# A chunk-streaming layer on one core: a new hand-written order for the mixed stages, with a re-fitted planner

## The chip, the cores and the metric

The kernel runs on one core of a Trainium2 chip. The metric is the device time of one execution in microseconds (us). The engines are TensorE (PE, with its weight loads shown apart as PEld), VectorE (DVE), ScalarE (ACT), GpSimd (POOL) and SyncE (SP), which here issues nearly all DMAs.

## The reference, cut to what matters

One layer of an encoder is computed for 512 prompt tokens and 32 sample tokens together (544 columns), in float32, with weights split in two rounded parts (high and low) so that each product takes three matmuls.

```python
xn = rms_norm(x, norm1)
q, k, v, iq, ik, iw, u, g_a, g_b = split(xn @ w_in)
# sparse attention: index scores, top-k keys per query, softmax over those keys
score = einsum(relu(iq . ik), iw);  top_k(score, n_sel);  o_a = softmax(q . k_sel) @ v_sel
# RWKV-7 time mixing: token shift, decay, a delta-rule state carried over chunks of tokens
y_b, shift_new, wkv_new = rwkv_time_mix(u, ...)
h = x + (sigmoid(g_a) * (o_a @ w_oa) + sigmoid(g_b) * (y_b @ w_ob)) @ w_out
h = h + (silu(rms_norm(h) @ w_gate) * (rms_norm(h) @ w_up)) @ w_down
y = rms_norm(h, norm_f)
```

Prompt queries choose 128 of up to 512 keys; sample queries choose 256 of 1056. The 16 index heads have 64 channels each; attention has 8 heads; the RWKV part has 8 heads, worked in four pairs.

## The kernel before, in words

Two kinds of work follow one another. In the *mixed stages* the input projection is done in 128-wide blocks, and between its matmuls lie all the small steps of attention and of RWKV. In the *late* part (merge, output projection, feed-forward) there are only large matmuls and their evictions.

**A weight block.** `wblock` (lines 246 to 265) loads 128 output columns of a weight matrix into one of two `raw` buffers (L255, a DMA on SP), copies the rounded high part with ACT (L256) and takes the low part with DVE (L260). Three `hi`/`lo` buffers go round. `gemm` multiplies a block with the 544 columns in two halves of 272, each 24 matmuls into one PSUM bank (L279), then evicts.

**The steps of the mixed stages.** `build` walks through the string `ORDER` (L67 to L70), whose words are steps, and emits each step's instructions:

- `U0` to `U3`: three projection blocks each for one RWKV pair (`u_pair`, `u_tile`, evictions L761 and L762, a shift on DVE at L767), stored to DRAM (L795). `L` is the first projection, of the LoRA inputs. From the word `U1` on, the projections use only PSUM banks 0 and 1.
- `P0` to `P3`: the preparation of one pair (`rwkv_prep`, L804 on), many small steps on every engine. `C0` to `C3`: the chain over nine chunks of tokens (`chain_step`, L1058 to L1071) and what follows it (`rwkv_post`, L1104 to L1143).
- `KV`, `IQ`, `Q`, `G0,16`: the projections of keys and values, index queries (eight blocks, stored to `iq_dram` at L467), queries (four blocks, stored to `q_dram` at L475) and gates (sixteen blocks, stored to `gate_dram` at L1150).
- `CI2`, `CI0,1`: cached keys of the sample stream brought in.
- `SI`: the sample index (`sample_index`, L477). After the scores it finds 256 keys per query by a bisection of 34 rounds (`topk_sample`); each round is a count on DVE (L529) and a small matmul over partitions (L530), and each waits for the one before.
- `X1` to `X3`: the selection for the second, third and fourth block of 128 prompt queries (`prompt_index`, L591): four query loads (L450, in `queries`), scores (L458, L459), relu on ACT (L604), a weighted sum over 16 heads on DVE (L611), then 16 rounds of a maximum of eight (L615) and a replacement (L616). The first block needs no selection. `FI` frees their buffers.
- `A0` to `A3`, `AS`: attention of the four prompt blocks and of the sample (`attend_prompt`, L629; scores with a maximum on DVE at L645; exponentials at L649; the output stored to `o_dram` at L680 except for the last). `UO`, `M`, `MA0`, `MA1`: the state output, the move to the merge, and the attention side of the merge for each half of the tokens.

**What shared buffers make of the order.** `queries` takes the next of two buffers (`qraw`, `qhs`) for its loads, and the scores take the next of two PSUM banks (`ab`). `SI`, `X`, `A`, `AS` and `CI` share them, in the order in which they are emitted. So the query loads of a step wait until the step emitted two loads earlier has used its own. `X1` to `X3` share one accumulator (`acc`), so each waits for the selection before it. `SI`, `A` and `AS` share the buffers `p_r` and `pT_r`, which `X` does not use.

**The planner.** The program is built twice. After the first build `plan` and `schedule` (L1602 on) run a list scheduling on the host: each instruction has a priority from the place where it was emitted plus a number of its group from the table `SHIFT` (lower goes first; a `w` before a name means that step's weight blocks), and costs, hand-over times between engines (`HOP`) and DMA times are constants in the file. The second build fixes the order that came out on each engine. `hold` and `keep` are added when PE would leave the full or a smaller tile shape; `turn` is added when an engine would change its starting partition, and where it is not in the table it is zero. Dependencies come from the emitted order, and the planner cannot go past them.

Of the kernel before, what the change touches and what calls it, by code (L numbers as in the profile page):

```python
# [35 lines left out]
def _consts():  # L36
# [28 lines left out]
B_COLS = 7432  # L65
ACT_COLS = 22 * 2 * T
ORDER = (  # L67
    "L U0 KV P0 IQ IA CI2 SI U1 P1 C0 X1 U2 P2 C1 Q A0 X2 U3 P3 C2 A1 CI0,1 AS X3 FI "
    "A2 G0,16 UO M MA0 C3 A3 MA1 "
)  # L70
SHIFT = {
# [7 lines left out]
    17100, "wstart": -230000,  # L79
}  # L80
BUSY = 1 << 40
AGE = 24
# [1385 lines left out]
def unlayout(r):  # L1468
# [6 lines left out]


HOP = {("PE", "Activation"): 200, ("PE", "DVE"): 200, ("PE", "Pool"): 225, ("DVE", "PE"): 149, ("Activation", "PE"): 160, ("Pool", "PE"): 174,
       ("Activation", "DVE"): 142, ("DVE", "Activation"): 128, ("DVE", "Pool"): 155, ("Activation", "Pool"): 210, ("Pool", "Activation"): 250,
       ("Pool", "DVE"): 70, ("DVE", "DVE"): 127, ("Pool", "Pool"): 104, ("Activation", "Activation"): 60, ("PE", "PE"): 0}
SECOND = {"PE": 54, "Activation": 70, "DVE": 70, "Pool": 48, "SP": 0}  # L1480
TURN = {"Activation": 128, "DVE": 110, "Pool": 112}
ENGINES = ("PE", "Activation", "DVE", "Pool", "SP")
WINDOW = 4096 / 1.2
ROUNDED, WHOLE, TURNED = 0, 1, 2
# [45 lines left out]
def side(i):  # L1530

    a = next((x for x in i.outs if hasattr(x, "ap")), None)
    step = list(a.ap)[0][0] if a is not None else 0
    return a.offset // step if step else 0


def port(i):
# [64 lines left out]
def plan(K, instructions):  # L1602

    at, group, g = {}, [], iter(K.groups + [(len(instructions), None)])
    block = [False] * len(instructions)
    for a, b in K.blocks:
        block[a:b] = [True] * (b - a)
    nxt, cur = next(g), "start"
    L, prio = [], []
    for n, i in enumerate(instructions):  # L1610
        while nxt and nxt[0] <= n:
            cur, nxt = nxt[1], next(g, None)
        if not i.opcode.startswith("Tile") and i.opcode != "Ldweights":
            at[i.name] = len(L)
            L.append(i)
            group.append(("w" if block[n] else "") + cur)
            prio.append(i.bass_priority + SHIFT.get(group[-1], 0))
    succ, need, reach = [[] for _ in L], [0] * len(L), []
    for k, i in enumerate(L):
        seen = 0  # L1620
        for p in sorted({at[x] for d in re.findall(r"deps=\[([^\]]*)\]", i.concise(deps=True)) for x in d.split(",") if x in at}, reverse=True):
            if p < k and not seen >> p & 1:
                succ[p].append(k)
                need[k] += 1
                seen |= reach[p] | 1 << p
        reach.append(seen)
    engine, dma, work = [str(i.engine)[11:] for i in L], [i.opcode == "DMACopy" for i in L], [cost(i) for i in L]
    sides = [0 if x or e in ("PE", "SP") else side(i) for x, e, i in zip(dma, engine, L)]
    return L, group, prio, succ, need, engine, dma, work, bundles(succ, group, engine, work, reach), sides


# [22 lines left out]
def schedule(L, group, prio, succ, need, engine, dma, work, runs, sides):  # L1654
    need, shared = list(need), [port(i) for i in L]
    missing, late, members = {}, {}, {}
# [4 lines left out]
    hold, keep, turn = SHIFT.get("hold", 0), SHIFT.get("keep", 0), SHIFT.get("turn", 0)  # L1661
    names = [e for e in ENGINES if e in engine]
    free, order, here = dict.fromkeys(names, 0.0), {e: [] for e in names}, {e: {} for e in names}
# [6 lines left out]
    array, queue, bus, left, at = Array(), 0.0, 0.0, len(L), dict.fromkeys(names, 0)  # L1670
# [22 lines left out]
    while left:  # L1693
# [3 lines left out]
        while coming and coming[0][0] <= t + 1e-6:  # L1697
            k = heapq.heappop(coming)[1]
# [4 lines left out]
        for e in names:  # L1703
            while free[e] <= t + 1e-6:
                if e == "PE":
# [4 lines left out]
                    k = heapq.heappop(tiles[best[1]])[1]  # L1710
                else:
# [3 lines left out]
                    k = heapq.heappop(here[e][best[1]])[1]  # L1715
# [8 lines left out]
                for p in before[k]:  # L1724
                    x, v = mark[p]
# [3 lines left out]
                t0 = max(t, ready[k] + SECOND[e]) if len(waits) > 1 else t  # L1729
                began = t0  # L1730
                if dma[k]:
                    queue = max(t0 + 67, queue + 25) + 450
                    bus = max(queue + 650, bus) + work[k]
                    end, free[e] = bus, t0 + 60
                elif isinstance(work[k], tuple):
                    began, end = array.run(t0, *work[k])
                    free[e] = max(began + 1, t0 + 1)
# [56 lines left out]
```

## Time and profile before

| what | value |
|---|---|
| median of 3 runs | 1007.6 us (1006.28 to 1008.33) |
| profiled execution, device time | 1007.89 us |
| its span, first to last instruction | 1006.1 us |
| mean granted TensorE clock | 0.985 |
| PE busy | 964.9 us, 96% of the span |
| DVE busy | 628.1 us, 62% |
| ACT busy | 460.0 us, 46% |
| POOL busy | 190.4 us, 19% |
| HBM traffic | 110 GB/s over the span |

The profiled execution lies 0.3 us above the median of the runs. Its device time holds 1.8 us outside the span. A share of busy time over the whole span mixes two parts: up to about 515 us the mixed stages run, after it the late part.

### The profile page before, as it was taken

What the parts mean: (1) busy time and instruction counts of PE and PEld (TensorE: products, weight loads), DVE (VectorE), ACT (ScalarE), POOL (GpSimd) and SP (SyncE); (2) the same over time, 40 slices, a digit from 0 to 9 for tenths busy, and PEclk for the clock granted to TensorE, in tenths of its full rate; (3) what the DMA queues carried; (4) which work ended last, traced back from release to release, by engine and by line L of the source; (5) the groups of instructions that cost most, each with busy time, mean ns of one, the idle gap of its engine ahead of it and who ended that gap; (6) DMA issues with size and microseconds to landing.
All of it is one profiled execution on the core that took longest, in us unless ns stands there. A gap on an engine that the chain in (4) does not pass through costs nothing.

```text
span 1006.1 us, 20829 instructions
## 1 busy us (share of the span) xinstructions
PE 964.9 (96%) x8268; PEld 923.4 (92%) x8268; DVE 628.1 (62%) x1452; ACT 460.0 (46%) x965; POOL 190.4 (19%) x307
## 2 busy tenths in 40 slices
PE   6989999999989999999999999999999999999996
PEld 5979997898879887899899999999999999999995
DVE  5947635999999898799677654444444444313132
ACT  6644555465546876565734452222323222223231
POOL 2212213322423421220000231111111111011112
PEclk9999999899999998999999999999999999999998
DMA  6246332432343455343555322232222233223222
GB/s 229 84 119 193 113 101 64 126 115 88 122 133 106 144 172 142 120 129 94 153 154 188 122 84 85 87 99 89 84 85 84 85 89 95 72 87 96 79 74 89
DMA packets 63282, 112.58 MB, mean 112 GB/s; under 512 B 13616, under 2 KB 33872, under 8 KB 63056
## 3 DMA queue, kind: packets, MB, share of 16 engines
q1 hardware_dynamic: 62144, 110.72, 35.7%
q8 instruction: 65, 1.06, 0.5%
q10 hardware_dynamic: 1040, 0.52, 0.2%
q14 instruction: 33, 0.27, 0.1%
HBM read 93.67 MB, written 17.14 MB: 110 GB/s over the span
## 4 chain that ended last, share of the span: by engine, by line
PE 72%; DVE 14%; DMA 6%; ACT 4%; issue 2%; SPq 1%; POOL 0%; DVEq 0%; ACTq 0%; POOLq 0%
PE bank L279 49%; PE bank L1330 13%; PE bank L458 1%; DVE w L260 1%; DVE f L616 1%; PE bank L459 1%; DMA iq_dram<-f 1%; DMA raw<-in_w_x_dram 1%; DVE f L611 1%; DVE f L615 1%; PE bank L901 1%; DVE f L529 1%; ACT w L256 1%; PE bank L1058 1%; DVE f L928 1%
## 5 line engine op out<-in xcount | busy, mean ns | idle before, releaser
L279 PE MATMUL bank<-r,w 128*128 128x272 f32 x4752 | 658.3, 293 | 3.2 <-ACT f L762 2.8
L279 PEld LDWEIGHTS bank<-r,w 128*128 128x128 f32 x4752 | 617.3, 189 | 10.0 <-ACT f L762 3.5
L256 ACT ACTIVATE w<-raw 128x1024 fp32r<-128x1024 f32 (+1 forms) x135 | 137.8, 1021 | 223.6 <-PE bank L279 172.7
L260 DVE TENSOR_TENSOR w<-raw,w 128x1024 fp32r<-128x1024 f32 (+1 forms) x135 | 176.5, 1308 | 97.8 <-ACT w L256 97.6
L1330 PE MATMUL bank<-r,w 128*128 128x272 f32 x1056 | 133.0, 288 | 0.0
L1330 PEld LDWEIGHTS bank<-r,w 128*128 128x128 f32 x1056 | 132.4, 188 | 0.0
L1308 POOL TENSOR_TENSOR f<-f 128x544 f32<-128x544 f32 x22 | 30.4, 1382 | 234.0 <-DVE f L1305 224.9
L1305 DVE TENSOR_TENSOR f<-bank,f 128x272 f32<-128x272 f32 x44 | 19.4, 442 | 74.8 <-PE bank L279 74.8
L1298 DVE TENSOR_TENSOR f<-bank,f 128x272 f32<-128x272 f32 x44 | 19.1, 435 | 45.1 <-PE bank L279 45.1
L453 POOL TENSOR_TENSOR k<-f,k 64x512 fp32r<-64x512 f32 (+1 forms) x22 | 30.1, 1372 | 49.0 <-ACT k L452 43.4
L458 PE MATMUL bank<-k 128*128 128x512 f32 (+5 forms) x102 | 35.8, 359 | 3.1 <-DVE f L645 1.3
L1332 DVE TENSOR_TENSOR f<-bank,f 128x272 f32<-128x272 f32 x16 | 7.1, 442 | 47.7 <-PE bank L1330 47.7
L1336 POOL TENSOR_TENSOR f<-f 128x272 f32<-128x272 f32 x13 | 12.4, 955 | 110.8 <-ACT f L1334 110.8
L459 PE MATMUL bank<-k 128*128 128x512 f32 (+5 forms) x102 | 33.0, 333 | 0.0
L1334 ACT ACTIVATE f<-f 128x272 f32<-128x272 f32 x16 | 6.8, 423 | 57.1 <-DVE f L1332 57.1
L1299 ACT ACTIVATE f<-f 128x272 f32<-128x272 f32 x44 | 18.7, 424 | 29.8 <-DVE f L1298 29.8
L611 DVE SCALAR_TENSOR_TENSOR f<-f,f 128x256 f32<-128x256 f32 (+2 forms) x45 | 31.7, 705 | 0.9 <-ACT f L604 0.3
L279 PE MATMUL bank<-k,w 128*128 128x272 f32 x144 | 22.8, 322 | 9.8 <-ACT k L300 9.8
L279 PEld LDWEIGHTS bank<-k,w 128*128 128x128 f32 x144 | 21.6, 219 | 10.1 <-ACT k L300 9.7
L458 PEld LDWEIGHTS bank<-k 128*128 128x128 f32 x102 | 19.1, 188 | 10.7 <-issue 5.1
L1074 POOL COPY f<-f 64x64 f32<-64x64 f32 x56 | 16.3, 292 | 65.3 <-DVE f L1071 63.9
L1250 POOL TENSOR_TENSOR f<-f 128x272 f32<-128x272 f32 x14 | 12.5, 896 | 75.3 <-DMA raw<-in_w_out_dram 51.7
(352 smaller groups left out, 1239.0 us busy)
## 6 DMA issues: line engine op xcount, KB each, us to landing
raw<-in_w_x_dram SPq DMA_DIRECT2D x41, 512.0 KB, 3.7
raw<-in_w_gate_dram SPq DMA_DIRECT2D x22, 512.0 KB, 3.6
raw<-in_w_up_dram SPq DMA_DIRECT2D x22, 512.0 KB, 3.6
raw<-in_w_down_dram SPq DMA_DIRECT2D x16, 512.0 KB, 3.6
gate_dram<-f SPq DMA_DIRECT2D x16, 272.0 KB, 2.4
raw<-in_w_oa_dram SPq DMA_DIRECT2D x8, 512.0 KB, 3.8
raw<-in_w_out_dram SPq DMA_DIRECT2D x8, 512.0 KB, 3.7
f<-iq_dram SPq DMA_DIRECT2D x26, 128.0 KB, 2.8
```

Of the source, the lines that this page charges most:

```text
L256: nc.scalar.activation(hi[:, a], raw[:, a], AF.Copy)
L260: self.lo_eng.tensor_tensor(lo[:, b], raw[:, b], hif[:, b], op=OP.subtract)
L279: nc.tensor.matmul(o, a[:, k], c[k][:, s], start=n == 0, stop=n == 3 * nk - 1)
L453: nc.gpsimd.tensor_tensor(ql[0:64], raw[0:64], qh_r.v(512)[0:64, :n], op=OP.subtract)
L458: nc.tensor.matmul(out, q[0][:, i:i + m], self.KS[:, j, keys], start=True, stop=False)
L459: nc.tensor.matmul(out, q[1][:, i:i + m], self.KS[:, j, keys], start=False, stop=stop)
L611: nc.vector.scalar_tensor_tensor(acc, r[:, i * S:(i + 1) * S], w, acc, op0=OP.mult, op1=OP.add)
L1298: nc.vector.tensor_tensor(t1[:, s], o, self.rs[:, s], op=OP.mult)
L1299: nc.scalar.activation(t1[:, s], t1[:, s], AF.Silu)
L1305: nc.vector.tensor_tensor(t2[:, s], o, self.rs[:, s], op=OP.mult)
L1308: nc.gpsimd.tensor_tensor(t1, t1, t2, op=OP.mult)
L1330: nc.tensor.matmul(o, a[:, k], c[k0 + k][:, s], start=m == 0, stop=m == 65)
```

## The change: what it does

In `ORDER` the second pair's projection `U1` stands ahead of the sample index `SI`; `X2` stands right behind `X1`, where it stood behind `A0`; `X3` and `FI` stand ahead of `U3`, `P3`, `C2`, `A1`, `CI0,1` and `AS`, where they stood behind `AS`. No step is added or taken away, and no instruction's shape changes.

All numbers of `SHIFT` are replaced, and `turn` is added. In the planner's model two hand-over times of GpSimd and one cost of a partition change are changed, and SP is taken as occupied for 330 ns by each DMA that it issues, 585 ns where one side of the copy has fewer than 128 partitions (60 ns before). Ready DMAs of the two kinds are queued apart.

```diff
 ORDER = (
-    "L U0 KV P0 IQ IA CI2 SI U1 P1 C0 X1 U2 P2 C1 Q A0 X2 U3 P3 C2 A1 CI0,1 AS X3 FI "
+    "L U0 KV P0 IQ IA CI2 U1 SI P1 C0 X1 X2 U2 P2 C1 Q A0 X3 FI U3 P3 C2 A1 CI0,1 AS "
     "A2 G0,16 UO M MA0 C3 A3 MA1 "
 )
 SHIFT = {
-    "A0": 230600, "A1": -4400, "A2": -703900, "A3": -225600, "AS": -582700, "C0": 247900, "C1": -1362900, "C2": -248200,
-    "C3": 114200, "CI0,1": 41500, "CI2": -198600, "G0,16": 2588600, "IA": 213400, "IQ": 1151100, "KV": -9600, "L": 65100,
-    "M": -200900, "MA0": 308900, "MA1": 123300, "P0": 259300, "P1": -250900, "P2": -372500, "P3": -86600, "Q": 3546000,
-    "R0": 299400, "R1": -1861400, "R2": -142400, "R3": 126400, "S": -59800, "SI": 126900, "U0": -21700, "U1": 1680300, "U2":
-    227900, "U3": 188000, "UO": -131400, "X1": 2420500, "X2": 24200, "X3": -241300, "hold": -55800, "keep": 2547100, "late":
+    "A0": 189800, "A1": -337800, "A2": 674100, "A3": -448400, "AS": -316200, "C0": 469200, "C1": -2295400, "C2": -279600,
+    "C3": -159300, "CI0,1": 8600, "CI2": -32700, "G0,16": 701400, "IA": 114200, "IQ": 1093000, "KV": -26200, "L": 224200,
+    "M": -330800, "MA0": 140200, "MA1": 187900, "P0": 1046500, "P1": -43900, "P2": -330500, "P3": -125000, "Q": 2748500,
+    "R0": 1376800, "R1": -861800, "R2": 525400, "R3": 38100, "S": -30900, "SI": 300400, "U0": 6700, "U1": 1510600, "U2":
+    802000, "U3": 296000, "UO": -13700, "X1": 2558100, "X2": -70800, "X3": -64500, "hold": -118500, "keep": 2716000, "late":
...
+    255500, "start": 407400, "turn": 87400, "wG0,16": 1072700, "wIQ": 155500, "wMA0": 1299200, "wMA1": -69900, "wP0": 18100,
...
-       ("Activation", "DVE"): 142, ("DVE", "Activation"): 128, ("DVE", "Pool"): 155, ("Activation", "Pool"): 210, ("Pool", "Activation"): 250,
-       ("Pool", "DVE"): 70, ("DVE", "DVE"): 127, ...
+       ("Activation", "DVE"): 142, ("DVE", "Activation"): 128, ("DVE", "Pool"): 155, ("Activation", "Pool"): 210, ("Pool", "Activation"): 112,
+       ("Pool", "DVE"): 110, ("DVE", "DVE"): 127, ...
-TURN = {"Activation": 128, "DVE": 110, "Pool": 112}
+TURN = {"Activation": 132, "DVE": 110, "Pool": 112}
...
+def narrow(i):
+    return any(list(x.ap)[0][1] < 128 for x in list(i.outs) + list(i.ins) if hasattr(x, "ap"))
...
-    sides = [0 if x or e in ("PE", "SP") else side(i) for x, e, i in zip(dma, engine, L)]
+    sides = [32 * narrow(i) if x else 0 if e == "PE" else side(i) for x, e, i in zip(dma, engine, L)]
...
-                    queue = max(t0 + 67, queue + 25) + 450
+                    issue = 585 if sides[k] else 330
+                    queue = max(t0 + 67, queue) + issue + 120
                     bus = max(queue + 650, bus) + work[k]
-                    end, free[e] = bus, t0 + 60
+                    end, free[e] = bus, t0 + (issue if e == "SP" else 60)
```

## Rows read from the trace of the kernel before

**Rows 1.** The page: busy time of the engines over the span, share, instructions

```profile
PE 964.9 (96%) x8268; PEld 923.4 (92%) x8268; DVE 628.1 (62%) x1452; ACT 460.0 (46%) x965; POOL 190.4 (19%) x307
```

**Rows 2.** Busy time by stretch: window, its length, then the columns named first

```profile
core 0: us, PE busy (x) PEld busy (x) DVE busy (x) ACT busy (x) POOL busy (x), PEclk, DMA share, GB/s
...
60.00:160.00 100.00, 95.19 (x903) 88.48 (x901) 52.93 (x139) 50.88 (x122) 20.46 (x38) 0.98 0.41 123
160.00:180.00 20.00, 15.74 (x112) 12.99 (x111) 17.43 (x39) 12.07 (x28) 9.49 (x16) 0.94 0.34 97
180.00:300.00 120.00, 113.01 (x1246) 103.69 (x1247) 114.10 (x415) 65.88 (x169) 35.68 (x79) 0.98 0.36 114
300.00:360.00 60.00, 59.03 (x504) 54.38 (x503) 53.95 (x143) 44.84 (x119) 24.82 (x47) 1.00 0.41 128
360.00:420.00 60.00, 56.44 (x602) 48.46 (x601) 49.86 (x146) 37.11 (x97) 8.01 (x9) 0.94 0.50 149
420.00:480.00 60.00, 59.92 (x455) 55.28 (x454) 56.92 (x135) 38.78 (x88) 13.20 (x19) 1.00 0.36 108
480.00:515.00 35.00, 34.61 (x273) 30.70 (x273) 26.19 (x51) 21.64 (x41) 1.95 (x1) 1.00 0.49 149
515.00:860.00 345.00, 345.00 (x2752) 345.00 (x2751) 176.76 (x254) 113.85 (x177) 42.76 (x37) 1.00 0.33 100
```

**Rows 3.** The same view for the large matmuls of L279 alone (PE, PEld)

```profile
20.00:515.00 495.00, 326.05 (x2111) 285.99 (x2110) 0.98 0.40 122
515.00:985.00 470.00, 345.78 (x2744) 344.77 (x2742) 1.00 0.31 95
```

**Rows 4.** The view of Rows 2 in short stretches around the idle places

```profile
175.00:180.00 5.00, 2.29 (x13) 1.76 (x14) 4.99 (x15) 3.98 (x11) 3.16 (x6) 0.77 0.72 203
180.00:185.00 5.00, 5.00 (x22) 4.80 (x23) 4.15 (x13) 1.26 (x5) 1.43 (x5) 0.55 0.31 107
...
385.00:390.00 5.00, 4.82 (x48) 3.81 (x49) 3.50 (x7) 3.22 (x9) 0.87 (x1) 0.59 0.58 157
390.00:395.00 5.00, 5.00 (x26) 3.86 (x25) 3.06 (x8) 0.85 (x2) 1.28 (x1) 0.73 0.90 269
...
280.00:300.00 20.00, 17.28 (x293) 15.75 (x294) 19.63 (x74) 8.32 (x23) 3.38 (x9) 1.00 0.42 133
```

**Rows 5.** Waits of PE, 155 to 182 us (us, times, longest); chain of waits there

```profile
PE bank L279 <- ACT f L762: 2.2, 1, 2.2
...
175.47 3.09 DMA u_dram<-f
```

**Rows 6.** One line's instructions: rounds of the sample index; stores of the gates

```profile
L529 DVE TENSOR_SCALAR_CACHE_REDUCE f<-f x34: 420/478/499, 172.0 to 297.5; 128x264 bf16<-128x264 f32 x34
...
L1150 SPq DMA_DIRECT2D gate_dram<-f x16: 319/326/553, 305.2 to 489.4; - x16
```

**Rows 7.** Timeline: first maximum of A0 on DVE, then the stores of attention

```profile
308.23 0.29 DVE L645 CUSTOM_DVE_ANT_0 f<-bank,f 128x128 f32<-128x128 f32 x1
...
341.62 0.39 SPq L680 DMA_DIRECT2D o_dram<-f  x1
...
417.04 0.37 SPq L680 DMA_DIRECT2D o_dram<-f  x1
...
463.84 0.37 SPq L680 DMA_DIRECT2D o_dram<-f  x1
```

**Rows 8.** The view of Rows 2 for the weighted sums of L611 alone (DVE)

```profile
340.00:380.00 40.00, 10.07 (x15) 1.00 0.49 146
...
420.00:440.00 20.00, 13.40 (x14) 1.00 0.36 97
```

**Rows 9.** DMAs of two tiles: duration on SP min/median/max ns, first and last start

```profile
L450 SPq DMA_DIRECT2D f<-iq_dram x26: 573/585/932, 94.6 to 410.1; - x26
...
L475 SPq DMA_DIRECT2D q_dram<-f x4: 319/321/332, 224.2 to 265.9; - x4
```

**Rows 10.** The page: the low part of a weight block on DVE

```profile
L260 DVE TENSOR_TENSOR w<-raw,w 128x1024 fp32r<-128x1024 f32 (+1 forms) x135 | 176.5, 1308 | 97.8 <-ACT w L256 97.6
```

More of the change, by code (lines that the diff above doesn't have):

```diff
@@ L71 @@
 SHIFT = {
[7 rows of a table removed]
-    17100, "wstart": -230000,
[7 rows of a table added]
+    146900, "wlate": 37400, "wstart": -36900,
 }
@@ L1477 @@
 HOP = {("PE", "Activation"): 200, ("PE", "DVE"): 200, ("PE", "Pool"): 225, ("DVE", "PE"): 149, ("Activation", "PE"): 160, ("Pool", "PE"): 174,
-       ("Activation", "DVE"): 142, ("DVE", "Activation"): 128, ("DVE", "Pool"): 155, ("Activation", "Pool"): 210, ("Pool", "Activation"): 250,
-       ("Pool", "DVE"): 70, ("DVE", "DVE"): 127, ("Pool", "Pool"): 104, ("Activation", "Activation"): 60, ("PE", "PE"): 0}
+       ("Activation", "DVE"): 142, ("DVE", "Activation"): 128, ("DVE", "Pool"): 155, ("Activation", "Pool"): 210, ("Pool", "Activation"): 112,
+       ("Pool", "DVE"): 110, ("DVE", "DVE"): 127, ("Pool", "Pool"): 104, ("Activation", "Activation"): 60, ("PE", "PE"): 0}
 SECOND = {"PE": 54, "Activation": 70, "DVE": 70, "Pool": 48, "SP": 0}
-TURN = {"Activation": 128, "DVE": 110, "Pool": 112}
+TURN = {"Activation": 132, "DVE": 110, "Pool": 112}
 ENGINES = ("PE", "Activation", "DVE", "Pool", "SP")
```

3 rows, old and new, of the table SHIFT are left out of this document.

## The prediction

> **What bounds the kernel now.** I read the shares of the page first: PE is busy 96% of the span and no other engine above 62% [rows 1]. That average hides two parts, which the windows by stretch tell apart [rows 2]. From 515 to 860 us PE is busy 345.00 of 345 us and DVE about half of it: the late part is a row of large matmuls, 345.78 us / 2744 = 126 ns each [rows 3], and no order can shorten it. Before 515 us PE has gaps, and there only can the change act. The idle time of PE, window minus busy: 4.81 us in 60 to 160, 4.26 in 160 to 180, 6.99 in 180 to 300, 0.97 in 300 to 360, 3.56 in 360 to 420, 0.08 in 420 to 480, 0.39 in 480 to 515 [rows 2]; 21.1 us in all. The large matmuls in that part show 326.05 / 2111 = 154 ns each [rows 3], 28 ns above the dense pace, 60 us in all. These are short waits behind small matmuls, which the busy share covers, so the idle time is not the whole of what an order can win or lose.
>
> Who makes PE wait? From 180 to 300 us DVE is busy 114.10 of 120 us, from 420 to 480 it is 56.92 of 60 [rows 2]: there it limits the rate at which weights are split and banks are emptied. From 60 to 160 us it is busy 52.93 of 100. The mixed stages are thus limited by DVE in their middle and by chains of dependent steps at their ends.
>
> Two places stand out. Between 160 and 180 us PE waits 2.2 us at one time for the eviction of a projection tile (L762), and the chain of waits goes there through a store of a projected row to `u_dram`, 3.09 us from issue to landing [rows 5]: the next tile's buffer came free only with it. PE is then at a granted clock of 0.77 and 0.55 from 175 to 185 us [rows 4]. Between 360 and 420 us there are several gaps, and the clock is 0.59 and 0.73 from 385 to 395 us.
>
> The second thing to see is a serial chain. The sample index runs its 34 rounds from 172.0 to 297.5 us, 3.7 us a round [rows 6], where the instruction itself takes 0.48 us; DVE has other work between. The first block's attention uses the same buffers, so its first maximum stands at 308.23 us; its output is stored at 341.62, that of the sample, with the second block's between them, at 417.04, that of the third block at 463.84 [rows 7]. The weighted sums of X2 lie inside this chain, 10.07 us of DVE in 340 to 380, and those of X3, 13.40 us in 420 to 440 [rows 8]. The last gate block is stored at 489.4 us [rows 6]; after it PE has little that does not hang on attention or on the last pair's chain.
>
> **The change part by part.** No instruction goes or comes, so every term is waiting.
>
> *U1 ahead of SI.* The rings of weight buffers see no new order, since SI has no weight block. What changes is who goes first on DVE, ACT and SP: the number of U1 falls by 169,700, that of SI rises by 173,500. The U1 tiles come out earlier against the index rounds, and this is the tile work that PE waits for at 160 to 180 us. The gap costs 4.26 us idle and, at the lower clock, (0.23 + 0.45) x 5 = 3.4 us [rows 2, 4], 7.7 us together. I take half, -3.8 us, since the tile's shift on DVE stays a neighbour of P1's steps. The ends: -7.7 (the gap goes) and +7.7 (a second such gap, since SI's start moves later and leaves PE without its scores).
>
> The lower clock follows the idle time in both places of [rows 4], and 280 to 300 us, with 2.72 us of idle in small pieces, keeps 1.00. The Trainium skill, page "TensorE: Matmul & The Clock Gate", Part 1, "What's actually happening", says that "the default state is throttled, and activity releases the throttle"; by it the two go together, as the trace shows. A reader who took the fall of the clock for a chance of this one execution would count only the idle halves of this part and the next, -2.1 and -1.8, and come to -1.4 us in the sum below.
>
> *X2 ahead of Q and A0.* Before, X2's loads stood in the two query buffers behind those of A0, which need `q_dram`, complete only after 265.9 us [rows 9]. Now X2 waits for `iq_dram` and for X1's accumulator alone. Its 8 loads (two per group, of 26 in all) take 585 ns each of SP [rows 9], 4.7 us; they move ahead of A0's loads and past weight loads on SP. A weight load held up by 4.7 us costs nothing as long as PE still has the block before it, 48 matmuls at 126 ns or 6.0 us; without that cover it costs the 4.7 us once. *X3 ahead of U3 to AS* moves 8 more such loads, and its 13.40 us of weighted sums, out of the stretch of 420 to 440 us. Between 360 and 420 us the selection of X2 leaves, and with it work of DVE that now stands beside P3 and the sample's attention. PE loses 3.56 us idle and (0.41 + 0.27) x 5 = 3.4 at the lower clock there [rows 2, 4], 7.0 together. I take half, -3.5 us; the ends are -7.0 and 0.
>
> *Where it comes back.* The work goes into 300 to 360 us, where DVE has 6 us left [rows 2]. I let PE's idle share rise there to that of 180 to 300 us, 6.99 / 120 = 5.8% of 60 us: 3.5 us for 0.97, so +2.5 us. The ends: 0, if X2 falls into the shadow of the sample index, and +10.07 us, if all its weighted sums stand in front of A0 and nothing behind takes advantage.
>
> *180 to 300 us* I leave at 0: DVE has 5.9 us left there and the same total of work. Ends +3.5 and -3.5, half of the idle time either way. *The late part*: 0, PE is full; only its start moves. *SP's new cost in the planner*: the rows show 585 ns for copies of 64 partitions and 320 for whole ones [rows 9], the new constants are these, and 60 was far off; a truer plan waits less, but no row prices it, so it stands in the ends above. *`turn`* keeps an engine on one starting partition; no row here shows such a turn by itself. I take 0, with ends of 0.5 us to either side, PE's whole idle time from 420 to 515 us [rows 2], the nearest that rows give for short hand-overs.
>
> The sum: -3.8 - 3.5 + 2.5 = -4.8 us. The profiled execution took 1007.89 us, so its like would take 1003.1; the median lies 0.3 us lower, which gives 1002.8 us.
>
> **The rivals.** *The gaps only move* (0 net, 1007.6 us). For it: DVE's total before 515 us is unchanged, and PE's gaps have small causes of many kinds, of which an order mends one and makes another. The priorities may also let the same instructions come out at the same places, the order of emission being only a bound; X1, whose number stays near 2.5 million, must still end before X2 may write the accumulator. Against it: 7.7 us sit in one place, and the store behind it belongs to the step that is moved.
>
> *The attention chain gets longer* (slower). One mechanism: SI starts behind U1's DVE work, some 6 us (three splits of 1.31 us [rows 10], and three shifts, taken at half to the whole of that, an estimate). A0 cannot begin before SI ends, A1 not before X3 has used the query buffers, and all that follows is serial up to the last block. After 489.4 us no gate projection is left to cover a later end [rows 6], so a delay of 6 us goes into the time whole: 1007.6 + 6 = 1013.6 us. It decides if SI's last round ends after about 304 us and the store of A2 after 463.84. Against it: X3's sums and selection no longer stand between AS and A3, so the tail can give 13.40 us back.
>
> *Both places close* (much faster): -7.7 - 7.0 - 3.5 + 2.5 = -15.7, 991.9 us. For it: X2 and X3 done early leave the attention steps without pauses. Against it: DVE is the bound in the middle and its work stays.
>
> **How the numbers follow.** The forecast 0.48, its own range 997 to 1005.5; gaps only move 0.21; chain longer 0.23; both places close 0.08. About 0.2%, 2 us, is what a measurement can tell from no change. Faster: 0.48 less a little for the edge of its range, plus 0.08, is 0.55; within 0.2% 0.21; slower 0.24. The range leaves out the far part of the last rival and the worst of the slower one: 994 to 1012 us.
>
> **What would show it.** Right: PE's idle time from 160 to 180 us (or wherever U1 ends) below 2.2 us with a clock of 1.00; X2's sums before 340 us and X3's before 400; the stores of the attention outputs closer together; the stretch without PE gaps beginning some us before 515. Wrong: SI's rounds ending after 304 us, a gap of over 3 us with a lower clock in 140 to 300 us, or a last gate block stored before 480 us with PE idle after it. If the forecast holds while X2 and X3 stand where they stood, the reason was another.

## The result, and the profile after

The changed kernel takes 1013.64 us in the median (1012.22 to 1014.86), the kernel before 1006.94 us beside it: 1.0066 of its time, 95% interval 1.0053 to 1.0079. The profiled executions, one of each, differ by 6.6 us of span (1012.7 for 1006.1). The forecast was 1002.8 us. Ratios are taken from executions timed beside one another, so they need not be the quotient of the medians shown, and one slow execution (1052.41 us at a mean clock of 0.843, of a_all below) is left out.

The page's line of busy time answers to [rows 1]:

```profile
PE 967.6 (96%) x8268; PEld 923.3 (91%) x8268; DVE 631.0 (62%) x1452; ACT 460.0 (45%) x965; POOL 195.6 (19%) x307
```

PE is busy 2.7 us more and idle 3.9 us more. The clock is not the reason: the mean granted clock was 0.986 to 0.990 in the four executions of the changed kernel, and of the 107 executions of the kernel before that were timed beside the experiments, the 65 in that range of clock took 1003.0 to 1009.7 us. By stretch, as [rows 2] (window, its length, busy time of PE, PEld, DVE, ACT, POOL, granted clock, DMA share, GB/s):

```profile
60.00:160.00 100.00, 96.98 (x919) 90.40 (x919) 54.55 (x146) 53.33 (x131) 21.70 (x39) 0.98 0.39 124
160.00:180.00 20.00, 16.06 (x110) 12.93 (x109) 18.86 (x49) 11.40 (x26) 8.29 (x15) 0.97 0.32 101
180.00:300.00 120.00, 112.54 (x1083) 102.64 (x1082) 110.27 (x389) 67.68 (x174) 41.48 (x79) 0.95 0.33 106
300.00:360.00 60.00, 57.28 (x607) 52.28 (x607) 56.77 (x153) 31.84 (x76) 17.40 (x37) 0.97 0.37 120
360.00:420.00 60.00, 56.73 (x628) 51.16 (x626) 56.22 (x145) 45.16 (x115) 16.27 (x19) 1.00 0.53 166
...
480.00:515.00 35.00, 35.00 (x255) 29.82 (x250) 25.22 (x57) 23.84 (x48) 2.83 (x1) 1.00 0.43 135
515.00:860.00 345.00, 342.74 (x2730) 342.34 (x2730) 178.56 (x257) 113.58 (x175) 42.78 (x37) 1.00 0.32 101
```

How far behind is the projection work when the late part starts? The same view for L279 alone, as [rows 3]:

```profile
20.00:515.00 495.00, 321.77 (x2087) 282.14 (x2086) 0.98 0.39 121
515.00:985.00 470.00, 350.17 (x2774) 348.76 (x2773) 1.00 0.31 97
```

After 515 us there are 30 more large matmuls than before, at 126 ns each 3.8 us of work that was not done in time. With the 2.26 us that PE now stands idle in 515 to 860 that makes 6.0 of the 6.6 us. So the loss has two parts in this pair of executions: 3.8 us are lost by 515 us, and 2.3 us behind it, where the kernel before lost nothing.

Of the 3.8 us, 2.8 are there before the first matmul. The timeline of PE, of ACT's copy of the second weight load and of SP's DMA issues at the start (start, duration, idle time before it and its releaser):

```profile
12.53 8.45 PE L279 MATMUL bank<-k,w 128*128 128x272 f32 x45 [12.53 <-ACT k L300]
...
10.49 0.63 ACT L256 ACTIVATE w<-raw 128x512 fp32r<-128x512 f32 x1 [5.15 <-DMA raw<-in_w_x_dram]
...
2.11 0.43 SPq L379 DMA_DIRECT2D f<-in_idx_k_g_dram  x1
2.58 0.43 SPq L380 DMA_DIRECT2D f<-in_idx_k_b_dram  x1
...
3.53 0.43 SPq L255 DMA_DIRECT2D raw<-in_w_x_dram  x1
4.01 3.39 SPq L296 DMA_DIRECT2D f<-in_x_t_dram  x4
```

The same of the kernel before, the first line from the page (busy, mean ns, idle time before the first matmul):

```profile
L279 PE MATMUL bank<-k,w 128*128 128x272 f32 x144 | 22.8, 322 | 9.8 <-ACT k L300 9.8
...
7.75 0.63 ACT L256 ACTIVATE w<-raw 128x512 fp32r<-128x512 f32 x1 [2.35 <-DMA raw<-in_w_x_dram]
...
9.84 0.33 SPq L379 DMA_DIRECT2D f<-in_idx_k_g_dram  x1
```

The first matmul stood at 9.75 us; the two broadcast loads of the index key's scale and offset (L379, L380) stood behind the loads of `x` and now stand ahead of them. From 20 to 515 us the rest of the change is worth +1.0 us net.

Inside that 1.0 us much moved. The short stretches behind the idle place of [rows 4], the second of them as it was before, then what DVE and PE did there in the changed kernel:

```profile
180.00:185.00 5.00, 4.00 (x18) 3.55 (x17) 2.21 (x7) 0.89 (x3) 0.89 (x2) 0.50 0.71 196
185.00:190.00 5.00, 4.26 (x19) 3.74 (x20) 4.73 (x18) 0.83 (x3) 2.66 (x7) 0.61 0.40 112
```

```profile
185.00:190.00 5.00, 5.00 (x41) 4.67 (x40) 4.78 (x21) 1.83 (x5) 1.87 (x4) 1.00 0.45 111
```

```profile
184.19 0.79 DVE L856 TENSOR_TENSOR f<-f 128x32 f32<-128x32 f32 x2 [2.50 <-DMA f<-u_dram]
...
185.74 2.18 PE L873 MATMUL bank<-f,f 128*128 128x272 f32 x4 [1.74 <-DVE f L870]
```

DVE stands idle for 2.50 us at the head of its queue: P1's first sum waits for the read-back of U1 from `u_dram`. The matmuls of L873 wait for it, and the clock is at 0.50 and 0.61 in these ten microseconds (0.55 and 1.00 before).

The index and the attention: as [rows 6] the rounds of SI and the stores of the gates, then as [rows 7] the first maximum of A0, and the first and the last of the stores of attention.

```profile
L529 DVE TENSOR_SCALAR_CACHE_REDUCE f<-f x34: 407/476/490, 171.5 to 360.6; 128x264 bf16<-128x264 f32 x34
...
L1150 SPq DMA_DIRECT2D gate_dram<-f x16: 319/323/593, 314.0 to 494.7; - x16
```

```profile
368.97 0.29 DVE L645 CUSTOM_DVE_ANT_0 f<-bank,f 128x128 f32<-128x128 f32 x1
...
390.14 0.39 SPq L680 DMA_DIRECT2D o_dram<-f  x1
...
485.01 0.37 SPq L680 DMA_DIRECT2D o_dram<-f  x1
```

SI starts where it did (171.5 us for 172.0), but its rounds are spread wider, 5.6 us a round for 3.7, so that it ends 63 us later than before and A0 starts 61 us later; the last store of attention is at 485.01 where it was at 463.84 [rows 7]. Yet PE is busy 35.00 of 35 us from 480 to 515. At 515 us begin the waits of the late part; the view of waits, then DVE's timeline there:

```profile
PE bank L279 <- DVE f L1194: 2.3, 2, 1.2
```

```profile
514.65 1.23 DVE L260 TENSOR_TENSOR w<-raw,w 128x1024 fp32r<-128x1024 f32 x1 [1.94 <-ACT w L256]
515.79 0.43 DVE L1194 SCALAR_TENSOR_TENSOR f<-f,bank 128x272 f32<-128x272 f32 x1
```

An eviction of the merge (L1194), which frees PE's bank, stands in DVE's queue behind a weight block's low part (L260), which itself waits for ACT and the block's load.

### The profile page after: what moved, and what is told of

It reads as the page before. It is cut to its first block, busy times and chain, and to the rows that moved or that the text cites. A ratio compares the mean times of both kernels' runs of the same rounds, so it can differ in the third digit from the quotient of the medians.

```text
span 1012.7 us, 20837 instructions
## 1 busy us (share of the span) xinstructions
PE 967.6 (96%) x8268; PEld 923.3 (91%) x8268; DVE 631.0 (62%) x1452; ACT 460.0 (45%) x965; POOL 195.6 (19%) x307
## 4 chain that ended last, share of the span: by engine, by line
PE 56%; DVE 8%; ACT 1%; DMA 1%; issue 1%; POOL 0%; DVEq 0%; ACTq 0%
PE bank L279 38%; PE bank L1330 13%; DVE w L260 1%; DVE f L616 1%; PE bank L458 1%; PE bank L459 1%; DMA raw<-in_w_ob_dram 0%; DVE f L615 0%; PE bank L661 0%; DVE f L645 0%; PE bank L727 0%; DMA raw<-in_w_oa_dram 0%; DMA b_dram<-f 0%; DVE f L611 0%; ACT f L649 0%
## 5 line engine op out<-in xcount | busy, mean ns | idle before, releaser
L279 PE MATMUL bank<-r,w 128*128 128x272 f32 x4752 | 658.5, 293 | 5.2 <-DVE f L1194 2.3
L279 PEld LDWEIGHTS bank<-r,w 128*128 128x128 f32 x4752 | 617.8, 190 | 11.8 <-issue 3.1
L260 DVE TENSOR_TENSOR w<-raw,w 128x1024 fp32r<-128x1024 f32 (+1 forms) x135 | 177.0, 1312 | 98.4 <-ACT w L256 98.2
L1074 POOL COPY f<-f 64x64 f32<-64x64 f32 x56 | 20.3, 362 | 79.9 <-DVE f L1071 77.3
L279 PE MATMUL bank<-k,w 128*128 128x272 f32 x144 | 21.7, 315 | 12.5 <-ACT k L300 12.5
L279 PEld LDWEIGHTS bank<-k,w 128*128 128x128 f32 x144 | 20.9, 214 | 12.5 <-ACT k L300 12.5
L611 DVE SCALAR_TENSOR_TENSOR f<-f,f 128x256 f32<-128x256 f32 (+2 forms) x45 | 31.4, 697 | 1.3 <-ACT f L604 0.6
```

Source lines behind the costliest of these rows:

```text
L260: self.lo_eng.tensor_tensor(lo[:, b], raw[:, b], hif[:, b], op=OP.subtract)
L279: nc.tensor.matmul(o, a[:, k], c[k][:, s], start=n == 0, stop=n == 3 * nk - 1)
L611: nc.vector.scalar_tensor_tensor(acc, r[:, i * S:(i + 1) * S], w, acc, op0=OP.mult, op1=OP.add)
L1074: nc.gpsimd.tensor_copy(QH[ps, cc + 1, e], ZV[e][ps, cc + 1])
```

## The experiments

Three theories. *Gaps*: PE is busy to the end, so each idle place costs about its length; the loss is the start, the place at 180 to 190 and the two evictions. *Chain*: the later index and attention set the end, as the slower rival had it. *Given back*: a place that is mended returns as another wait.

All experiments but two keep the planned order and move a few instructions of one engine's queue (the numbers are positions in the program as emitted). The edit is always this, with other triples:

```diff
-    nc = program(arrays, schedule(*plan(K, instructions)))[0]
+    order = schedule(*plan(K, instructions))
+    for engine, moved, behind in (
+        ('SP', [416, 417], 32),
+    ):
+        q = order[engine]
+        for k in moved:
+            q.remove(k)
+        at = q.index(behind) + 1
+        q[at:at] = moved
+    nc = program(arrays, order)[0]
```

**The start alone** (a_start, the edit above: L379 and L380 behind the last load of `x`).

> The changed kernel with its planned order kept, except that SP issues the two broadcast loads of the index key's scale and offset (L379, L380) behind the loads of x, where the kernel before has them, instead of ahead of them. First matmul back at about 9.8 us (12.5 in the changed kernel). Theory 'gaps' (PE is busy to the end, so what it loses at one place it never gets back; the start is 2.8 of the 6.7 us): 1010.9 us, about 1.004 of the kernel before. Theory 'chain' (the index and attention steps that run later decide): 1013.6, 1.0066, since none of them starts earlier. Third theory 'given back' (the late start is made up by fewer idle places in 60-160, where the changed kernel has 3.0 us of idle PE against 4.8): 1012.5 to 1013.6, and the idle time in 60-160 goes back up by about what the start gains.

Measured: 1009.83 us, 1.0028 of before (1.0012 to 1.0044). The first matmul is back:

```profile
9.74 7.81 PE L279 MATMUL bank<-k,w 128*128 128x272 f32 x45 [9.74 <-ACT k L300]
```

Two small loads in front of a queue cost 3.8 us of the 6.7, somewhat more than the 2.8 us of the first matmul; the rest is within the interval, and this interval lies clear of the changed kernel's. Chain expected none of it. PE's waits for the evictions L1194, which this edit does not touch, are smaller here too, 1.4 us in all for 2.3.

**The place at 182 us alone** (a_gap).

```diff
+        ('DVE', [1877, 1878, 1890], 1685),
+        ('PE', [1891, 1893], 2543),
```

> The changed kernel with its planned order kept, except at one place: VectorE does P1's three operations that wait for the u_dram load (L856 twice, L870) behind the next seven of its queue, and PE does L873 behind the nine matmuls of L279 that follow it. In the changed kernel VectorE stood idle 2.5 us there (181.7 to 184.2), PE 1.7 us, and the granted clock was 0.50 and 0.61 in 180-190. 'Gaps': both close, 1.7 us of idle and up to 4 us of clock come back: 1008 to 1012, 1.001 to 1.005 of the kernel before. 'Chain': one round of the bisection comes about 3 us earlier, but PE's and VectorE's order behind it is the same, so 1013.6 or up to 1 less. 'Given back': 1012.5 to 1014, with the idle time at a later wait between 185 and 300.

Measured: 1011.63 us, 1.0054 (1.0038 to 1.0070). The clock of the ten microseconds is whole, the idle time is not less (1.72 us for 1.74), and ahead of the place, from 160 to 180 us, the clock is 0.91 for 0.97:

```profile
180.00:185.00 5.00, 4.45 (x28) 3.45 (x26) 4.80 (x17) 0.89 (x2) 1.16 (x4) 1.00 0.60 166
185.00:190.00 5.00, 3.83 (x25) 3.22 (x26) 4.07 (x21) 2.07 (x7) 2.10 (x6) 1.00 0.60 175
```

The direction is that of gaps, but the interval overlaps that of the changed kernel (1.0053 to 1.0079): by itself this is not settled.

**The two evictions alone** (a_evict).

```diff
+        ('DVE', [5512], 5498),
+        ('DVE', [5853], 5836),
```

> The changed kernel with its planned order kept, except that on VectorE two evictions of the merge (L1194) go ahead of a weight block's low part (L260) that waits for ScalarE and for the block's load. In the changed kernel PE waits at these two evictions at 515-516 and 524-525, 2.3 us in all, which the kernel before does not have. 'Gaps': 1011.4, 1.0044 of the kernel before, and 515-860 without idle PE. 'Chain' (the attention's end at 512 decides, and the waits are its trace): the low part was on the path, so a wait for a weight block takes their place: 1013 to 1014.

Measured: 1010.88 us, 1.0044 (1.0026 to 1.0062), where gaps put it. This interval, too, overlaps that of the changed kernel, so by itself this is not settled either. PE still waits once in the late part, 0.8 us for L1194, where it waited 2.3: the trace shows 1.5 us less, and part of that can come without the edit, as a_start shows. No wait for a weight block took the place, so the low part was not on the path; it only stood in front.

**The three together** (a_all).

> The changed kernel with the three edits together: the two loads at the start behind x, P1's three operations and L873 moved back at 182-186, and the two evictions at 515-525 ahead of the low parts. 'Gaps': the sum of the three, 2.8 + 1.7 to 5 + 2.3 us: 1003.5 to 1007, 0.997 to 1.000 of the kernel before, so level with it or ahead. 'Chain': 1012 to 1014. 'Given back': 1009 to 1012, only the last place counting in full since nothing but large matmuls follows it.

Measured: 1006.67 us, 1.0010 (0.9997 to 1.0023): level with the kernel before, at the edge of what gaps expected, and clear of the changed kernel. By the ratios the three edits alone took off 0.38, 0.12 and 0.22% of the time, together they take off 0.56: the sum is larger, but within the intervals. What the index does in this kernel, and the large matmuls as in [rows 3]:

```profile
L529 DVE TENSOR_SCALAR_CACHE_REDUCE f<-f x34: 407/476/490, 167.6 to 355.5; 128x264 bf16<-128x264 f32 x34
```

```profile
20.00:515.00 495.00, 323.55 (x2113) 284.03 (x2112) 0.98 0.39 122
515.00:985.00 470.00, 345.32 (x2740) 344.31 (x2738) 1.00 0.30 95
```

SI ends at 355.5 us, 58 us later than before, and the time is the same: chain has fallen. The backlog at 515 us is gone (2113 large matmuls for 2111). One wait for L1194, of 1.1 us, is left; it lies ahead of 515 us now.

**The start, put into the kernel before** (b_start, the mirror).

```diff
+        ('SP', [416, 417], 1393),
```

> The kernel before with its planned order kept, except that SP issues the two broadcast loads of the index key's scale and offset (L379, L380) ahead of the loads of x, where the changed kernel has them: the mirror of a_start, which took 3.8 us off the changed kernel. 'Gaps' (lost at the start, never made up): first matmul at about 12.5 us instead of 9.75 and 1009.5 to 1011, 1.0027 to 1.004 of the kernel before. 'Given back' (the kernel before has a 3.2 us wait of PE at 66.75 for VectorE's L406, which a later start may fill): 1007 to 1008, and the wait at 66 shorter by 2 to 3 us. 'Chain': no change.

Measured: 1008.22 us, 1.0024 (1.0003 to 1.0046). PE's timeline:

```profile
12.62 7.65 PE L279 MATMUL bank<-k,w 128*128 128x272 f32 x40 [12.62 <-ACT k L300]
...
68.21 0.33 PE L432 MATMUL bank<-f,f 128*128 128x128 f32 x1 [3.12 <-DVE f L406]
```

The wait for L406 keeps its length (3.12 us for 3.2), so the late start is not made up there; but it comes 1.46 us later, not 2.87, so half was made up between the two. The trace is that of the fastest of the twelve executions (1005.56 us), and by 515 us this execution has nothing left of the late start (2725 large matmuls still to do, for 2744 in the kernel before). The cost in the ratio, 2.4 us, lies between the two theories' numbers and nearer to gaps; the interval covers both, and no cost is just outside it.

**The order without the numbers, and the numbers without the order** (order_only and tables_only, both planned anew). The first is the kernel before with the new `ORDER` string, the second the changed kernel with the old one:

```diff
-    "L U0 KV P0 IQ IA CI2 SI U1 P1 C0 X1 U2 P2 C1 Q A0 X2 U3 P3 C2 A1 CI0,1 AS X3 FI "
+    "L U0 KV P0 IQ IA CI2 U1 SI P1 C0 X1 X2 U2 P2 C1 Q A0 X3 FI U3 P3 C2 A1 CI0,1 AS "
```

> The new ORDER string with all numbers and constants of the planner as before (a new plan). 'The order is worse': 1011 to 1015, as the changed kernel. 'The order is better or the same, the numbers lost the time': 1000 to 1008. 'Order and numbers are fitted to one another': slower than both kernels, over 1015, with many more waits of PE over 0.5 us in 60-515 than either has.

> The ORDER string of before with the new SHIFT and the planner's new constants (a new plan). 'The order is worse': 1003 to 1008. 'The numbers lost the time': 1011 to 1015, with the first matmul at 12.5 us as in the changed kernel. 'Fitted to one another': slower than both kernels, over 1015.

Measured: 1030.77 us, 1.0237 (1.0212 to 1.0263), and 1033.96 us, 1.0265 (1.0237 to 1.0293). Each half alone loses some 25 us, together they lose 6.7. The page's line of busy time and the first matmul in the timeline, of the order alone:

```profile
PE 978.0 (95%) x8268; PEld 929.6 (90%) x8268; DVE 632.5 (61%) x1452; ACT 459.5 (45%) x965; POOL 188.6 (18%) x307
```

```profile
9.33 7.86 PE L279 MATMUL bank<-k,w 128*128 128x272 f32 x43 [9.33 <-ACT k L300]
```

And of the numbers alone:

```profile
PE 983.2 (95%) x8268; PEld 938.1 (90%) x8268; DVE 629.7 (61%) x1452; ACT 458.5 (44%) x965; POOL 196.6 (19%) x307
```

```profile
12.45 7.81 PE L279 MATMUL bank<-k,w 128*128 128x272 f32 x45 [12.45 <-ACT k L300]
```

Order and numbers are fitted to one another. PE is idle some 10 and 13 us more in the profiled executions and busy 13 and 18 us more; the busy part is the clock's: in stretches of 5 us from 20 to 515, (1 - clock) times the length adds up to 23.9 and 29.0 us, for 10.2 in the kernel before. And the late start goes with the numbers and constants, not with the order: it is there with the old order and absent with the new one. Which of the numbers or of the planner's SP cost moves the two loads was not tried apart.

**More mends on top of a_all** (a_more). Can the new order then be made faster than the kernel before?

```diff
+        ('Activation', [2207, 1514, 1544, 1570, 2304, 2311, 1545, 1571], 2578),
+        ('DVE', [1669, 1675, 2209, 1670, 2210], 2579),
+        ('Activation', [2664, 2690, 2665, 2691], 2634),
+        ('DVE', [5791], 5809),
```

> a_all with four more moves in ScalarE's and VectorE's queues, all of one kind: evictions and small steps that PE waits for go ahead of a weight block's rounding (L256) or low part (L260) that waits for its load or its buffer. At 170-178 (U1's last evictions L761 and L762, X1's relu L604 and C0's steps ahead of the second block's rounding; a_all has 4.3 us of idle PE at its waits there), at 213-215 (U2's evictions; 1.7 us), at 509-512 (one L1194; 1.1 us). 'Gaps': 3 to 6 us less than a_all, 1001 to 1004.5, 0.994 to 0.998 of the kernel before: faster than both kernels. 'Given back': 1006 to 1008, the same idle time at other places between 170 and 300.

Measured: 1015.09 us, 1.0083 (1.0058 to 1.0107): 8 us worse than a_all. ACT's timeline, the store of U1's second tile on SP, and PE:

```profile
174.60 0.69 ACT L761 ACTIVATE f<-bank 128x272 f32<-128x272 f32 x2 [3.78 <-DMA u_dram<-f]
...
172.17 0.38 SPq L795 DMA_DIRECT2D u_dram<-f  x1
...
175.83 0.58 PE L458 MATMUL bank<-k 128*128 128x256 f32 x1 [4.71 <-ACT f L604]
```

The eviction L761 writes into a stage buffer that is free only when the store of an earlier tile has landed, 2.4 us behind its issue. (The Trainium skill, "DMA: Bandwidth & Descriptors", "Latency and other measured facts", puts the fixed cost of a DMA at about 2 us, most of it the receipt round trip to the target memory; the 2.4 us here are the whole time from issue to landing, and no run splits them.) Moved ahead of L604 it put that wait in front of what PE wanted: one wait of 4.7 us where a_all had three, of 3.1, 0.5 and 0.9, and behind it one of 2.7 us for C0's L1060. From 160 to 190 us PE is idle 8.6 us for 5.9 in a_all, and (1 - clock) times the length is 6.8 us for 3.4: some 6 us together, as much as the spans of the two profiled executions differ (1011.9 for 1005.8). That the wait for the store alone did it is not shown: the other moves of this run were not tried apart.

**The same place without the hidden wait** (a_more2).

```diff
+        ('Activation', [2207, 1514, 2304, 2311], 2578),
+        ('Activation', [2352], 1571),
+        ('Activation', [2215], 1571),
+        ('DVE', [1669, 1675, 2209, 1670, 2210], 2579),
+        ('SP', [1515], 1656),
```

> a_all with another set of moves around 168 to 178, after a_more had set U1's last evictions (L761) ahead of X1's relu (L604) and so a wait for the store of U1's second tile ahead of it. Now ScalarE does C0's L1063, L768 and X1's two L604 ahead of the second block's rounding (L256), and U1's evictions ahead of one query copy (L452) that waits for its load; VectorE does five small steps ahead of that block's low part (L260); SP issues the store of U1's second tile (L795) ahead of a weight load that waits for its buffer. PE waits in a_all at 173.47 for 3.1 us, 174.41 for 0.5 and 177.65 for 0.9. 'Gaps': these shrink by 2 to 3 us and the clock of 175-185 rises with them: 1003.5 to 1005.5, 0.997 to 0.999 of the kernel before. 'Given back': 1006 to 1008, with the same idle time moved to 178-230. 'A hidden wait again': over 1009, with one wait of PE over 3 us in 168-185.

Measured: 1006.90 us, 1.0003 (0.9989 to 1.0017). The waits of 4.5 us became 3.3, of which this is the largest:

```profile
176.80 0.43 PE L1061 MATMUL bank<-f,f 128*128 128x64 f32 x2 [2.91 <-ACT f L1060]
```

In the trace the wait was partly given back: PE does its steps in a fixed order, and the chain of C0 behind the mended wait became the next one; from 160 to 190 us PE is idle 4.8 us for 5.9. The time cannot tell this from nothing, nor from a part of what gaps expected: the interval reaches down to 0.9989.

**The same kind of move in the kernel before** (b_more).

```diff
+        ('SP', [1770], 1474),
+        ('Activation', [2352], 1826),
```

> The kernel before with its planned order kept, except for two moves of the same kind: SP issues the store of U1's second tile (L795) between the second and the third of SI's four L506 copies instead of behind them and a weight load, and ScalarE does U1's last evictions (L761, L762) ahead of one query copy (L452). In the kernel before PE waits 2.2 us at 179.76 for L762, and L761 had waited for that store. 'Gaps': 1.5 to 2 us less, 1004.5 to 1005.5, 0.998 to 0.999 of the kernel before. 'Given back': no change, with the wait at 179.76 shorter and another one behind it longer. 'A hidden wait again': slower by 1 us or more.

Measured: 1006.68 us, 1.0003 (0.9989 to 1.0018). The wait for L762 of [rows 5] fell from 2.2 to 0.8 us; no gain in the time can be told, though the interval still holds the 0.999 of gaps.

**Filling PE's short idle places** (a_fill, b_fill, a_fill2). Matmuls of the running projection go ahead of a small one that waits: in seven places on top of a_more2 (with two further moves), in four on top of b_more, and, after the first had left a new wait, in six of the seven alone. One triple of each kind:

```diff
+        ('PE', [4546, 4547, 4548, 4549, 4550, 4551], 4545),
...
+        ('PE', [4547, 4548, 4549, 4550], 4546),
```

> a_more2 with PE's idle places filled: at seven waits of PE between 230 and 400 (0.69, 1.20, 0.95, 0.95, 0.73, 0.83 and 0.73 us, 6.1 in all, each for a small step of P1, P2, P3, X2, C2 or R2) four to eight matmuls of the projection that already runs go ahead of the waiting one instead of behind it. Besides, at 173-177 C0's L1059 and L1060 go ahead of the second block's low part and of U1's evictions (PE waits 2.9 us at 176.80 in a_more2), and at 213 U2's last evictions ahead of one query copy (1.7 us at 214.43). 'Gaps' (an idle place costs its length, wherever it is): 6 to 8 us less than a_more2, 999 to 1001, 0.992 to 0.994 of the kernel before: faster than both kernels. 'Given back' (the projections run out earlier, or a filled place makes its chain late, so other waits grow): 1004 to 1007.

> b_more with four idle places of the kernel before filled in the same way: at the waits of PE before L901 of P0 (0.69 us at 99.2), L1007 of P2 (0.60 at 299.9), L458 of A1 (1.25 at 374.6) and L1007 of P3 (0.64 at 381.4), 3.2 us in all, four to seven matmuls of the running projection go ahead of the waiting one. 'Gaps': 3 us less than b_more, 1003 to 1004.5, 0.996 to 0.998 of the kernel before. 'Given back': 1006 to 1007.

> a_more2 with six of the seven fillings of a_fill and nothing else: four to six matmuls of the running projection go ahead of the waiting one at 230.6, 306.4, 363.0, 385.3, 388.6 and 399.4 (0.69, 0.95, 0.95, 0.73, 0.83 and 0.73 us, 4.9 in all). Left out are the filling at 296.2, behind which a_fill had a new wait of 1.8 us for a weight block's low part (L260), and the moves at 173-177 and 213, whose waits had come back as others. 'Gaps' (what a_fill lost was its three other edits): 3.5 to 5 us less than a_more2, 1002 to 1003.5, 0.995 to 0.9965 of the kernel before. 'Given back' (a filled short place makes the projections' next block or the small chain late, or the hand-overs dearer): 1005.5 to 1007.5, 0.999 to 1.001.

Measured: 1007.62 us, 1.0002 (0.9982 to 1.0022); 1006.80 us, 1.0008 (0.9979 to 1.0037); 1008.06 us, 1.0015 (0.9991 to 1.0039). None gained what gaps said; for the first and the last it lies outside the interval, for the second (0.998 at the least) at its very edge. In the first, the filling at 296 us met a weight block whose low part was not ready:

```profile
296.95 1.27 PE L279 MATMUL bank<-r,w 128*128 128x272 f32 x8 [1.81 <-DVE w L260]
```

The last one, without it, from 180 to 420 us, and a_more2 under it:

```profile
180.00:300.00 120.00, 113.44 (x1228) 102.16 (x1228) 112.70 (x386) 71.14 (x181) 41.00 (x80) 0.99 0.34 107
300.00:360.00 60.00, 58.15 (x504) 53.98 (x504) 58.41 (x162) 31.01 (x75) 19.04 (x38) 1.00 0.34 116
360.00:420.00 60.00, 57.71 (x627) 51.26 (x626) 56.45 (x149) 46.33 (x121) 15.76 (x19) 1.00 0.55 165
```

```profile
180.00:300.00 120.00, 112.42 (x1158) 100.70 (x1156) 112.54 (x390) 70.15 (x179) 41.44 (x80) 0.99 0.34 107
300.00:360.00 60.00, 57.70 (x565) 53.47 (x566) 58.42 (x162) 31.86 (x78) 18.51 (x38) 1.00 0.37 120
360.00:420.00 60.00, 56.64 (x624) 50.49 (x623) 56.17 (x148) 44.70 (x116) 15.43 (x18) 1.00 0.56 166
```

PE's idle time falls from 13.2 to 10.7 us, 2.5 of the 4.9 that were filled; the profiled execution's span falls by 1.5 us (1003.5 for 1005.0), the median does not. A gain of 3.5 us or more is outside the interval. Whether the 2.5 us come back in time at all stays open: where ten executions or more of one kernel were timed, they lie 5 to 13 us apart, and the medians tell about 2.

## Why the prediction was wrong

Two steps of the sum failed, about equally. From 20 to 515 us it promised -4.8 us, and the large matmuls show +1.0. And what lies outside the moved steps it put at nothing, where 5.1 us were lost.

*The bookkeeping of the new plan outside the moved steps.* The prediction priced what the moved words of `ORDER` do, and set "the late part: 0, PE is full", had no term for the start, and put the planner's new SP cost "in the ends" because "no row prices it". There lie 2.8 us before the first matmul and 2.3 us in 515 to 860. a_start shows the first by itself, and its mirror agrees; a_evict points to the second without settling it; a_all shows that these two places and the one at 182 us are the loss. No row of before could give the new queue orders; but the diff said that SP would be planned by another cost, and the first matmul stands behind loads that SP issues. A range for that belonged into the sum. Whether this cost or the numbers of `SHIFT` moved the two loads stays open.

*U1 ahead of SI*, forecast -3.8 us in 160 to 180. The wait that the term was built on, 2.2 us for L762 [rows 5], is gone. In its place PE waits for steps of C0 and for P1's read-back; the view of its waits from 160 to 190 us:

```profile
PE bank L1061 <- ACT f L1060: 2.5, 2, 1.4
PE bank L873 <- DVE f L870: 1.7, 1, 1.7
PE bank L1064 <- ACT f L1063: 0.8, 1, 0.8
```

The idle time of 160 to 190 us is 5.7 us for 4.3, and (1 - clock) times the length, in stretches of 5 us, 5.1 us for 3.4: 3.1 us lost in all where 3.8 were to be won. The clock's share varies from execution to execution (3.4 us in a_start, where this place is as in the changed kernel); the idle time does not. This is the rival of the moved gaps, at this one place; the prediction named the transfer of U1 for its store and not for the read-back, which is what DVE then waited for.

*X2 and X3 moved*, forecast -3.5 in 360 to 420: the number came, -3.7 us, but not by the mechanism. The idle time is 3.27 us for 3.56; the work of DVE did not leave (busy 56.22 us for 49.86), since X3's sums came where X2's had been. The weighted sums of L611 on DVE:

```profile
280.00:320.00 40.00, 10.93 (x15) 1.00 0.37 116
...
380.00:420.00 40.00, 13.26 (x15) 1.00 0.62 193
```

What was won is the clock, 1.00 for 0.94. That is in part luck: in all nine traces of the changed kernel and of its edits with the planned order kept it is 1.00 there, but of those of the kernel before it is 0.94 in the unedited one and in b_more, 0.97 in b_fill and 1.00 in b_start. *Where it comes back*, forecast +2.5 in 300 to 360: right in kind, with 1.75 us more idle time here and 1.3 to 2.9 in the other such traces without fillings. The clock of 0.97 adds 1.7 us in this execution; a_start and a_all have 1.00 there.

*The rivals.* The longer chain gave 1013.6 us, which is the time that was measured, and its condition was met: SI ended after 304 us, and the last store of attention came after 463.84. Its mechanism is not what happened: SI did not start later, as it had it, and PE was full up to 515 us, because the gates run until 494.7 us beside the attention; a_all ends level with SI still 58 us late. A rival that hits the number can be wrong. The range, up to 1012 us, left out the time of this rival, which had a chance of 0.23. *Gaps only move* is what the middle of the kernel did.

Idle time and (1 - clock) times the length, summed over the stretches of 5 us from 20 to 515, would make this part 0.9 us shorter than before (20.65 + 10.25 for 21.58 + 10.2 us); the large matmuls say 1.0 us longer. The 1.9 us between lie in the busy time, in short waits behind small matmuls if the clock tells all of its part, and no run here placed them.

## What to carry to other kernels

When a hand-written order and a planner's numbers change together, price the new plan at the places where one queue alone decides: the first loads, and evictions that stand behind a preparation which itself waits. Test such a plan with its order fixed and one instruction moved; planning anew moves everything, by 25 us here. Idle time of an engine is worth its length only where nothing else is about to become late: here the start was, the two evictions perhaps, and eleven short places were not, as far as the medians can tell.

## What the runs showed of the hardware

Two broadcast loads, 0.43 us of SP each, ahead of `x` delayed the first matmul by 2.8 us, three times their issue time. The second weight load was issued 0.94 us later (3.53 for 2.59) and then took longer: ACT, which waits for it ahead of its steps on `x`, began to copy it 7.0 us after its issue, for 5.2 before. The third weight load was issued 3.95 us later (9.68 for 5.73). Why the second load took longer, no run here shows.

In a_gap the same idle time as in the changed kernel, 1.7 us in 180 to 190, went with a whole clock, while the stretch ahead of it, 160 to 180, was at 0.91 for 0.97; in a_start, which does not touch this place, 180 to 190 was at 0.95 and 0.71 for 0.50 and 0.61. Which stretch is at the lower of the clock's two levels (0.50 here) follows the idle time only loosely, by these rows.

The clock goes with much of the spread between executions of one kernel. Of the 107 executions of the kernel before, the 23 with a mean granted clock of 0.989 or more took 1005.6 us in the median, the 20 with 0.983 or less 1009.7 us.
